# Two transformer-like layers on one core: the first modulation with its loads in another order, four column groups and products of zeros

## The chip, the cores and the metric

One Trainium2 chip, one NeuronCore of it. The metric is the device time of one execution in microseconds (us). The engines are PE (TensorE, matrix products), DVE (VectorE), ACT (ScalarE), POOL (GpSimd) and SP (SyncE, which issues all of the loads and stores here).

## The reference

A backbone of two layers over 256 context tokens and 512 latent tokens, 1024 channels each. Each layer starts with a norm whose scale and shift are computed from a conditioning vector (the modulation); four token mixers, gates, an output projection and an MLP follow. What the change touches is the first of these lines in layer 0, and the first two column blocks of the projection (the Fourier branch, fn):

```python
mod_l = (silu(c) @ ada_w[l] + ada_b[l])[:, None, :]
mod_c = (silu(c_ctx) @ ada_w[l] + ada_b[l])[None, None, :]
sh1, sc1, g1, sh2, sc2, g2 = jnp.split(mod_l, 6, axis=-1)
def rms_norm(x, w):
    return x * lax.rsqrt(jnp.mean(x * x, axis=-1, keepdims=True) + NORM_EPS) * w
def ada_rms(x, w, shift, scale):
    return rms_norm(x, w) * (1.0 + scale) + shift
hc = ada_rms(xc, norm_mix_w[l], csh1, csc1)
hl = ada_rms(xl, norm_mix_w[l], sh1, sc1)
z = h @ w_in[l]
```

## The kernel before

Activations stand transposed: eight tiles `self.x[k]` of 128 channels by 768 tokens (256 context, 512 latent). Every large product is made of three fp32r products of high and low halves, `hhi,wlo`, `hlo,whi` and `hhi,whi` (`gemm`, L311): for each of eight k it streams 256 and 512 columns. `split` (L296) makes the halves of a weight chunk, the high one on ACT and the low one on DVE. After the start the kernel is one long stream of such products on PE, through all branches of both layers; most of ada_w is not multiplied on PE but on DVE, later (`ada`, L567).

`start` (L500 to L565) is the stage in question. It computes the part of the modulation that layer 0's first norm needs, in four calls `modulation(i)` of 512 output columns each: 8 and 12 are the two halves of the scale, 0 and 4 those of the shift. A call takes eight weight tiles `adp` (128 x 512 fp32, 256 KB) from DRAM and multiplies each with two columns of `csil`, silu(c) and silu(c_ctx) of 128 channels (L514). The result, 2 x 512 in PSUM, is copied to `adt` by ACT (L516), transposed by four PE transposes (L518), and added to the bias by DVE into `mod` (L519); for the scale, `ada_fin` makes `am` of it. `mid` is a table of things to do ahead of a tile: the x tiles are loaded between the weight tiles, each followed by its square on ACT and its sum over k on POOL (`sumsq`, L597), `tables` loads constants and stores csil to DRAM as `crow` (L537, element by element), and `scalars` does the DVE work of `s5_scalars` (L1348), parameters of a later branch that are written to DRAM as `par`.

`norm_stat` (L628) sums the squares over channels by six products with a column of ones, takes a reciprocal root on DVE in eleven small steps, and spreads it over partitions by six transposes (`rs_y`). `norm_apply` (L609) then makes `hhi` (ACT) and `hlo` (DVE) per k from x, am, mod and that tile. The first two fn products (`self.head`) run on the halves k = 0 to 3 and are completed later in `fnet`, with k = 4 to 7. The first Fourier product behind them reads the constant `c_f`.

PSUM has two buffers named `b` (`pb`, L328) that the modulations and the norm share, and two named `mm`. `adp` has 16 buffers. The order of instructions on an engine is written by the framework's scheduler, starting from the order of the program; all DMAs go through SP's queue, over eight semaphores in turn, and one DMA waits for the eighth before it.

Of the kernel before, what the change touches and what calls it, by code (L numbers as in the profile page):

```python
# [10 lines left out]
F32 = mybir.dt.float32  # L11
F32R = mybir.dt.float32r
# [3 lines left out]
OP = mybir.AluOpType  # L16
# [5 lines left out]
KT = 8  # L22
# [3 lines left out]
DEPTH = 2  # L26
# [132 lines left out]
PRM_MAIN = PRM_OFF['qkk'][1]  # L159
# [56 lines left out]
class Net:  # L216
# [27 lines left out]
    def mm(self, out, a, b, start, stop):  # L244
        return self.nc.tensor.matmul(out, a, b, start=start, stop=stop)  # L245
# [59 lines left out]
    def mm3(self, out, a, b, start, stop):  # L305

        self.mm(out, a[1], b[0], start, False)
        self.mm(out, a[0], b[1], False, False)
        self.mm(out, a[0], b[0], False, stop)
# [190 lines left out]
    def start(self, sp, prm):  # L500

        nc = self.nc
        m = self.mod[0]

        def modulation(i, mid={}):

            p = self.pb()
            for k in range(KT):
                if k in mid:
                    mid[k]()  # L510
                r = sp.tile([128, 512], F32, name="adp", bufs=16)
                o, n = self.off[('adp', i, k)]
                nc.sync.dma_start(r, bass.AP(tensor=self.wst.tensor, offset=self.wst.offset + o, ap=[[n, 128], [1, n]]))
                self.mm(p[:2, :512], self.csil[:, k], r, k == 0, k == KT - 1)  # L514
            t = sp.tile([2, 512], F32, name="adt", bufs=2)
            self.act(t, p[:2, :512])  # L516
            for j in range(4):
                self.tr(p[:, 512 + 2 * j:514 + 2 * j], t[:, 128 * j:128 * j + 128], 2)  # L518
            self.tt(m[:, i:i + 4], p[:, 512:520].rearrange("p (i v) -> p i v", i=4),  # L519
                    self.main[0]['ada_b'][:, i:i + 4, None].to_broadcast([128, 4, 2]), OP.add)  # L520
            self.ada_fin(0, i, 4)

        def load():
            j = len(done)
            done.append(j)
            nc.sync.dma_start(self.x[j], self.xT[j])
            self.sumsq(sp, j, both, nc.gpsimd)

        both = [CTX, LAT]
        self.ss = {}  # L530
        done = []
        def tables():
            nc.sync.dma_start(self.ident, self.cst_ap('ident'))
            for l in range(DEPTH):
                nc.sync.dma_start(prm[l], self.prm[l][:, :PRM_MAIN])
            for v in range(2):
                nc.sync.dma_start(self.crow[v].rearrange("(k p) -> p k", p=128), self.csil[:, :, v])  # L537

        def scalars():
            for _ in range(8):  # L540
                next(later)

        later = self.s5_scalars(0, sp)
        st = []

        def stat():
            st.append(self.norm_stat(both, self.ss[0]))
            next(st[0])

        modulation(8, {2: scalars, 3: load, 5: load, 7: tables})  # L550
        modulation(0, {0: load, 2: load, 4: load, 6: load})
        self.h = self.halves()
        modulation(12, {0: load, 2: load, 6: stat})
        self.fetch(('A', 0, 'fn', 0), ('A', 0, 'fn', 1), eng=nc.vector)
        nb = next(st[0])
        modulation(4)
        self.norm_apply(0, 0, both, nb, range(4))
        self.head = []
        for j in range(2):
            self.head.append((self.pmm(), self.wk(self.chunk(('A', 0, 'fn', j)), KT)))  # L560
            self.gemm(*self.head[j], self.h, both, range(4))
        self.norm_apply(0, 0, both, self.np, range(4, 8))
        with self.tc.issue_after(self.last.ins):
            for _ in later:
                pass  # L565

# [1165 lines left out]
```

## Time and profile before

| | us |
|---|---|
| median of 3 runs | 2182.86 (2182.38 to 2184.0) |
| the profiled execution | 2183.58 |
| its span, first to last instruction | 2181.8 |
| PE busy in it | 2132.3 |
| mean granted clock of PE | 0.996 |

The span is the time from the first to the last instruction on the core; the profiled execution's time is 1.8 us longer. Busy times are sums over an engine's instructions. The clock is given as a share of PE's full 2.4 GHz; its lower level, 0.50, is 1.2 GHz.

### The profile page before, as it was taken

To read this page: it belongs to the slowest core of one execution; us is meant where nothing else is said; L and a number is where in the kernel's file an instruction comes from. 1 tells how busy PE (TensorE), PEld (TensorE's weight loads), DVE (VectorE), ACT (ScalarE), POOL (GpSimd) and SP (SyncE) were. 2 spreads that over 40 slices of the span, in tenths; PEclk is the share of its full clock that TensorE was granted. 3 is DMA by queue.
4 is the path that set the end of the run, shared out by engine and by line. 5 is a ranking of instruction groups with operands and counts; after the bars stand their busy time and mean duration, and the time that the engine had idled before them with its cause. 6 is when DMAs were issued, how large, how long until landed. Compare 5 with 4: busy or idle time off the path is not lost.

```text
span 2181.8 us, 32131 instructions
## 1 busy us (share of the span) xinstructions
PE 2132.3 (98%) x12366; PEld 1819.4 (83%) x12366; DVE 1418.9 (65%) x3303; ACT 793.7 (36%) x1346; POOL 60.9 (3%) x95
## 2 busy tenths in 40 slices
PE   6999999999999999999999999999999999999999
PEld 1888988888888888888888888997888779888887
DVE  5977789965735476667885457567646656444444
ACT  2422434564434232221222235435644544223322
POOL 2001000000000000000000001100000001000000
PEclk8999999999999999999999999999999999999999
DMA  8444233414324145445242232122144352333332
GB/s 273 148 130 131 78 103 115 144 34 130 93 73 150 36 150 159 167 134 183 100 125 82 88 118 78 40 59 80 53 123 120 112 152 60 98 96 94 96 98 94
DMA packets 117768, 239.93 MB, mean 110 GB/s; under 512 B 16208, under 2 KB 45552, under 8 KB 117616
## 3 DMA queue, kind: packets, MB, share of 16 engines
q1 hardware_dynamic: 117616, 237.89, 35.2%
q8 instruction: 97, 1.59, 0.3%
q14 instruction: 55, 0.45, 0.1%
HBM read 218.29 MB, written 19.55 MB: 109 GB/s over the span
## 4 chain that ended last, share of the span: by engine, by line
PE 79%; DVE 7%; ACT 2%; issue 2%; DMA 1%; POOL 1%; SPq 0%; POOLq 0%; ACTq 0%; DVEq 0%
PE mm L245 49%; PE b L245 27%; PE b L248 3%; DVE wlo L300 1%; DVE olo L497 1%; ACT tmp L264 1%; POOL hlo L251 0%; DVE xy L261 0%; ACT whi L299 0%; DVE ob L251 0%; DMA raws<-wst 0%; DVE gate L261 0%; DVE tmp L251 0%; DMA ohi<-crow 0%; DMA raw<-wst 0%
## 5 line engine op out<-in xcount | busy, mean ns | idle before, releaser
L245 PE MATMUL mm<-hhi,wlo 128*128 128x256 f32 (+1 forms) x1768 | 534.3, 356 | 1.1 <-DVE kr L1226 0.4
L245 PE MATMUL mm<-hlo,whi 128*128 128x256 f32 (+1 forms) x1768 | 531.5, 354 | 3.6 <-POOL hlo L251 3.5
L245 PE MATMUL mm<-hhi,whi 128*128 128x256 f32 (+1 forms) x1768 | 530.8, 354 | 0.0
L300 DVE TENSOR_TENSOR wlo<-raw,whi 128x1024 fp32r<-128x1024 f32 (+2 forms) x233 | 282.4, 1212 | 150.6 <-ACT whi L299 150.4
L245 PEld LDWEIGHTS mm<-hlo,whi 128*128 128x128 f32 x1768 | 332.2, 188 | 52.8 <-POOL hlo L251 6.5
L245 PEld LDWEIGHTS mm<-hhi,wlo 128*128 128x128 f32 x1768 | 329.8, 188 | 49.5 <-issue 1.3
L245 PEld LDWEIGHTS mm<-hhi,whi 128*128 128x128 f32 x1768 | 332.1, 188 | 46.2
L299 ACT ACTIVATE whi<-raw 128x1024 fp32r<-128x1024 f32 (+2 forms) x233 | 243.2, 1046 | 344.5 <-PE b L245 295.1
L261 DVE SCALAR_TENSOR_TENSOR xy<-b,mod,xy 128x256 f32<-128x256 f32 (+1 forms) x192 | 121.9, 659 | 147.3 <-PE b L245 147.0
L245 PE MATMUL b<-uh,wlo 128*128 128x256 f32 (+1 forms) x704 | 215.0, 359 | 2.4 <-DVE xy L261 1.3
L245 PE MATMUL b<-ul,whi 128*128 128x256 f32 (+1 forms) x704 | 214.5, 357 | 0.6 <-DVE ul L300 0.6
L245 PE MATMUL b<-uh,whi 128*128 128x256 f32 (+1 forms) x704 | 214.9, 357 | 0.0
L264 ACT ACTIVATE tmp<-mm 128x768 f32<-128x768 f32 (+3 forms) x86 | 51.5, 598 | 300.9 <-PE mm L245 281.9
L251 DVE TENSOR_TENSOR tmp<-tmp 128x768 f32<-128x768 f32 (+1 forms) x64 | 52.8, 825 | 162.0 <-ACT tmp L264 162.0
L245 PEld LDWEIGHTS b<-uh,wlo 128*128 128x128 f32 x704 | 131.2, 188 | 26.6 <-ACT uh L299 4.7
L245 PEld LDWEIGHTS b<-ul,whi 128*128 128x128 f32 x704 | 131.9, 188 | 22.3 <-DVE ul L300 1.6
L245 PEld LDWEIGHTS b<-uh,whi 128*128 128x128 f32 x704 | 132.1, 188 | 19.5
L245 PE MATMUL mm<-whi,hlo 128*128 128x256 f32 (+1 forms) x424 | 122.6, 289 | 1.1 <-DVE rpt L261 0.7
L245 PE MATMUL mm<-wlo,hhi 128*128 128x256 f32 (+1 forms) x424 | 122.1, 288 | 1.1 <-DVE wlo L300 1.1
L245 PE MATMUL mm<-whi,hhi 128*128 128x256 f32 (+1 forms) x424 | 121.9, 287 | 0.0
L264 ACT ACTIVATE gate<-mm 128x768 f32<-128x768 f32 (+1 forms) x64 | 45.0, 703 | 169.2 <-PE mm L245 168.9
L497 DVE CUSTOM_DVE_ANT_0 adu<-adr,adc 128x512 bf16<-128x512 f32 x128 | 88.2, 689 | 3.3 <-DMA adr<-wst 0.6
(454 smaller groups left out, 3183.9 us busy)
## 6 DMA issues: line engine op xcount, KB each, us to landing
raw<-wst SPq DMA_DIRECT2D x236, 512.0 KB
adr<-wst SPq DMA_DIRECT2D x96, 256.0 KB
olo<-wst SPq DMA_DIRECT2D x42, 256.0 KB
adp<-wst SPq DMA_DIRECT2D x32, 256.0 KB
raws<-wst SPq DMA_DIRECT2D x64, 128.0 KB
xy<-xT SPq DMA_DIRECT2D x16, 384.0 KB
ohi<-wst SPq DMA_DIRECT2D x22, 256.0 KB
oB<-scr SPq DMA_DIRECT2D x16, 294.0 KB
```

What stands on the lines that cost most here:

```text
L245: return self.nc.tensor.matmul(out, a, b, start=start, stop=stop)
L248: self.nc.tensor.transpose(out, a, self.ident[:n, :n])
L251: (eng or self.nc.vector).tensor_tensor(out=out, in0=a, in1=b, op=op)
L261: (eng or self.nc.vector).scalar_tensor_tensor(out, a, s, b, op0=op0, op1=op1)
L264: self.nc.scalar.activation(out, a, f, **kw)
L299: self.last_hi = self.nc.scalar.activation(hi, src, AF.Copy)
L300: return (eng or self.nc.vector).tensor_tensor(out=lo, in0=src, in1=hi.bitcast(F32), op=OP.subtract)
L497: self.nc.vector.tensor_tensor_reduce(out=junk, in0=r, in1=c[:, v], scale=1.0, scalar=0.0, op0=OP.mult, op1=OP.add, accum_out=acc[:, v:v + 1])
```

## The change

The x tiles are loaded first, then constants, the two fn weight chunks and the parameters of `s5_scalars`, then all weight tiles of the modulation. The sums of squares move from POOL to DVE. The norm's statistics are computed ahead of the modulations, in the order 8, 0, 12, 4, and between 0 and 12 `norm_apply` for k = 0 to 3 and the first half of both fn products. silu(c) is padded with zeros to 32 columns (`c32`), and tile k writes rows 32 (k mod 4) and up of PSUM; the four groups are added by a product with `sel`, four identity pieces of two columns, which also transposes. After every weight tile two fp32r products of zeros, 128 x 128 by 128 x 512, are written to an unused half of the same PSUM tile. crow is transposed on PE and stored as rows of 128 numbers, after everything else of the stage.

```diff
@@ -502,65 +502,74 @@
         nc = self.nc
         m = self.mod[0]
 
-        def modulation(i, mid={}):
+
+        c32 = sp.tile([128, KT, 32], F32, name="c32")
+        nc.gpsimd.memset(c32, 0.0)
+        self.act(c32[:, :, 0:2], self.csil)
+        sel = sp.tile([128, 2], F32, name="sel")
+        zero = sp.tile([128, 512], F32, name="zero")
+        nc.gpsimd.memset(zero, 0.0)
+        zr = sp.tile([128, 512], F32R, name="zr")
+        self.act(zr, zero)
+
+        def modulation(i):
 
             p = self.pb()
             for k in range(KT):
-                if k in mid:
-                    mid[k]()
                 r = sp.tile([128, 512], F32, name="adp", bufs=16)
                 o, n = self.off[('adp', i, k)]
-                nc.sync.dma_start(r, bass.AP(tensor=self.wst.tensor, offset=self.wst.offset + o, ap=[[n, 128], [1, n]]))
-                self.mm(p[:2, :512], self.csil[:, k], r, k == 0, k == KT - 1)
-            t = sp.tile([2, 512], F32, name="adt", bufs=2)
-            self.act(t, p[:2, :512])
+                self.last = nc.sync.dma_start(r, bass.AP(tensor=self.wst.tensor, offset=self.wst.offset + o, ap=[[n, 128], [1, n]]))
+                g = 32 * (k % 4)
+                self.mm(p[g:g + 32, :512], c32[:, k], r, k < 4, k >= 4)
+
+                for _ in range(2):
+                    self.mm(p[:, 512:], zr[:, :128], zr, True, True)
+            t = sp.tile([128, 512], F32, name="adt", bufs=2)
+            self.act(t, p[:, :512])
             for j in range(4):
-                self.tr(p[:, 512 + 2 * j:514 + 2 * j], t[:, 128 * j:128 * j + 128], 2)
+                self.mm(p[:, 512 + 2 * j:514 + 2 * j], t[:, 128 * j:128 * j + 128], sel, True, True)
             self.tt(m[:, i:i + 4], p[:, 512:520].rearrange("p (i v) -> p i v", i=4),
                     self.main[0]['ada_b'][:, i:i + 4, None].to_broadcast([128, 4, 2]), OP.add)
             self.ada_fin(0, i, 4)
 
-        def load():
-            j = len(done)
-            done.append(j)
-            nc.sync.dma_start(self.x[j], self.xT[j])
-            self.sumsq(sp, j, both, nc.gpsimd)
-
         both = [CTX, LAT]
         self.ss = {}
-        done = []
-        def tables():
-            nc.sync.dma_start(self.ident, self.cst_ap('ident'))
-            for l in range(DEPTH):
-                nc.sync.dma_start(prm[l], self.prm[l][:, :PRM_MAIN])
-            for v in range(2):
-                nc.sync.dma_start(self.crow[v].rearrange("(k p) -> p k", p=128), self.csil[:, :, v])
-
-        def scalars():
-            for _ in range(8):
-                next(later)
-
+        for k in range(KT):
+            nc.sync.dma_start(self.x[k], self.xT[k])
+            self.sumsq(sp, k, both)
+        nc.sync.dma_start(self.ident, self.cst_ap('ident'))
+        self.tt(sel, self.ident[:, 0:2], self.ident[:, 32:34], OP.add)
+        for g in (64, 96):
+            self.tt(sel, sel, self.ident[:, g:g + 2], OP.add)
+        for l in range(DEPTH):
+            nc.sync.dma_start(prm[l], self.prm[l][:, :PRM_MAIN])
+        self.fetch(('A', 0, 'fn', 0), ('A', 0, 'fn', 1))
         later = self.s5_scalars(0, sp)
-        st = []
-
-        def stat():
-            st.append(self.norm_stat(both, self.ss[0]))
-            next(st[0])
-
-        modulation(8, {2: scalars, 3: load, 5: load, 7: tables})
-        modulation(0, {0: load, 2: load, 4: load, 6: load})
+        next(later)
+        st = self.norm_stat(both, self.ss[0])
+        next(st)
+        modulation(8)
         self.h = self.halves()
-        modulation(12, {0: load, 2: load, 6: stat})
-        self.fetch(('A', 0, 'fn', 0), ('A', 0, 'fn', 1), eng=nc.vector)
-        nb = next(st[0])
-        modulation(4)
+        nb = next(st)
+        modulation(0)
         self.norm_apply(0, 0, both, nb, range(4))
         self.head = []
         for j in range(2):
             self.head.append((self.pmm(), self.wk(self.chunk(('A', 0, 'fn', j)), KT)))
             self.gemm(*self.head[j], self.h, both, range(4))
-        self.norm_apply(0, 0, both, self.np, range(4, 8))
+        modulation(12)
+        modulation(4)
+        self.norm_apply(0, 0, both, nb, range(4, 8))
+        for _ in range(7):
+            next(later)
+        p = self.pb()
+        rows = sp.tile([8, 2, 128], F32, name="crows")
+        for v in range(2):
+            self.tr(p[:8, 128 * v:128 * v + 128], self.csil[:, :, v])
+        self.act(rows, p[:8, :256])
         with self.tc.issue_after(self.last.ins):
+            for v in range(2):
+                nc.sync.dma_start(self.crow[v].rearrange("(k p) -> k p", p=128), rows[:, v])
             for _ in later:
                 pass
```

How this moves instructions shows at three places. First PE at the head of the program, before: `adp` are the weight tiles, `adt` the evicted rows, `ss` the sum of squares, `rs_y` the reciprocal root.

```order
L245 MATMUL b<-adp,csil 2x512 x8
L248 MATMUL b<-ident,adt 128x2 x4
L245 MATMUL b<-adp,csil 2x512 x8
L248 MATMUL b<-ident,adt 128x2 x4
L245 MATMUL b<-adp,csil 2x512 x6
L245 MATMUL b<-ones,ss_298 128x1 x6
L245 MATMUL b<-adp,csil 2x512 x2
L248 MATMUL b<-ident,rs_y 128x128 x4
```

And the same engine now, from its first product to the end of the first modulation (the pair of a tile and two products with `zr` stands eight times; three of them are shown, and what ends and follows them):

```order
L245 MATMUL b<-ones,ss_109 128x1 x6
L248 MATMUL b<-ident,rs_y 128x128 x6
L245 MATMUL b<-adp,c_100 32x512
L245 MATMUL b<-zr 128x512 x2
L245 MATMUL b<-adp,c_100 32x512
L245 MATMUL b<-zr 128x512 x2
...
L245 MATMUL b<-zr 128x512 x2
L245 MATMUL b<-sel,adt 128x2 x4
L245 MATMUL b<-adp,c_100 32x512
```

The norm's products now come before every modulation product, each tile is followed by two products of zeros, and four products with `sel` stand where four transposes did.

Second, PE where modulation 0 ends now, with the waits of each row (DVE_49 and Activation_49 are the counters of DVE and ACT, DMAHW those of loads):

```order
L245 MATMUL b<-sel,adt 128x2 [waits Activation_49]
L245 MATMUL b<-sel,adt 128x2 x3
L245 MATMUL b<-adp,c_100 32x512 [waits DMAHW2_49,DVE_49]
L245 MATMUL mm<-hhi_239,wlo 128x256 [waits Activation_49]
L245 MATMUL mm<-hhi_239,wlo 128x256
L245 MATMUL b<-zr 128x512
L245 MATMUL mm<-hhi_239,wlo 128x512 [waits Activation_49]
L245 MATMUL mm<-hlo_240,whi 128x256 [waits DVE_49]
```

The first tile of modulation 12 has moved ahead of the fn products and waits for DVE; the other seven stand behind the 48 fn products of k = 0 to 3. Before, all 32 tiles stood ahead of the first fn product.

Third, SP's queue: the rows around the crow stores before,

```order
L535 DMA prm_72<-prm 128x69 [waits DMAHW0_49]
L537 DMA crow<-csil 128x8x1 [waits DMAHW1_49,DVE_49]
L537 DMA crow<-csil 128x8x1 [waits DMAHW2_49]
L513 DMA adp<-wst 128x512 [waits DMAHW3_49]
L526 DMA xy_91<-xT 128x768 [waits DMAHW4_49]
L513 DMA adp<-wst 128x512 [waits DMAHW5_49]
```

and around their new place, behind all modulation tiles:

```order
L521 DMA adp<-wst 128x512 [waits DMAHW1_49,PE_49]
L270 DMA raw<-wst 128x1024 [waits DMAHW2_49,DVE_49]
L1421 DMA par_80<-par 128x1616 [waits DMAHW3_49,DVE_49]
L270 DMA raw<-wst 128x1024 [waits DMAHW4_49,Activation_49]
...
L572 DMA crow<-crows 8x128 [waits DMAHW0_49,Activation_49]
L572 DMA crow<-crows 8x128 [waits DMAHW1_49]
L465 DMA c_f_700<-cst 128x256 [waits DMAHW1_49,DMAHW0_49,DMAHW3_49,PE_49,Pool_49]
L1431 DMA par<-par_80 128x1616
```

The stores of crow have moved from between the weight tiles to just ahead of `c_f` and the load of `par`, and wait for ACT there.

## Rows read from the trace of the kernel before

**Rows 1.** The page, part 1: busy us, share of the span, instructions per engine.
```profile
PE 2132.3 (98%) x12366; PEld 1819.4 (83%) x12366; DVE 1418.9 (65%) x3303; ACT 793.7 (36%) x1346; POOL 60.9 (3%) x95
```
**Rows 2.** Windows by stage: us; PE, PEld, DVE, ACT, POOL busy; clock, DMA share, GB/s.
```profile
0.00:72.00 72.00, 54.06 (x190) 22.52 (x191) 47.83 (x211) 24.43 (x39) 13.55 (x16) 0.91 0.71 228
72.00:200.00 128.00, 123.89 (x850) 107.36 (x849) 101.83 (x311) 38.95 (x86) 3.33 (x7) 1.00 0.49 143
```
**Rows 3.** Waits of PE in 0 to 72: us in total, times, longest.
```profile
PE b L245 <- DMA adp<-wst: 15.3, 5, 8.9
```
**Rows 4.** Timeline, SP's issues and PE: start, us, engine, line, what, [idle before].
```profile
1.17 0.89 SPq L513 DMA_DIRECT2D adp<-wst  x2
...
4.23 3.57 PE L245 MATMUL b<-adp,csil 128*2 128x512 f32 x4 [4.23 <-DMA adp<-wst]
...
10.48 1.01 SPq L537 DMA_DIRECT2D crow<-csil  x2
...
16.92 5.16 SPq L513 DMA_DIRECT2D adp<-wst  x2
...
23.60 1.87 PE L245 MATMUL b<-adp,csil 128*2 128x512 f32 x2 [8.94 <-DMA adp<-wst]
```
**Rows 5.** Windows of 2 us, columns as in rows 2: clock and load rate.
```profile
24.00:26.00 2.00, 1.47 (x2) 0.00 (x0) 1.92 (x12) 0.50 (x2) 0.00 (x0) 0.50 1.00 386
...
30.00:32.00 2.00, 2.00 (x4) 0.34 (x3) 0.00 (x0) 0.49 (x2) 1.92 (x2) 0.60 1.03 390
...
36.00:38.00 2.00, 1.32 (x8) 0.49 (x7) 0.17 (x1) 1.83 (x3) 0.37 (x1) 1.00 1.05 387
```
**Rows 6.** Timeline of PE, 37 to 73.
```profile
37.14 5.31 PE L245 MATMUL b<-adp,csil 128*2 128x512 f32 x12
42.38 1.50 PE L245 MATMUL b<-ones,ss 128*128 128x1 f32 x12
43.81 1.88 PE L245 MATMUL b<-adp,csil 128*2 128x512 f32 x4
46.16 0.65 PE L248 MATMUL b<-ident,rs_y 128*128 128x128 f32 x4 [0.47 <-DVE rs_y L261]
...
47.08 0.43 PE L248 MATMUL b<-ident,rs_y 128*128 128x128 f32 x2
47.48 7.03 PE L245 MATMUL b<-adp,csil 128*2 128x512 f32 x16
54.44 0.62 PE L245 MATMUL mm<-hhi,wlo 128*128 128x256 f32 x2
54.89 0.51 PE L245 MATMUL mm<-hlo,whi 128*128 128x256 f32 x2
55.25 0.51 PE L245 MATMUL mm<-hhi,whi 128*128 128x256 f32 x2
...
72.92 1.34 PE L245 MATMUL b<-c_f,u 128*128 128x128 f32 x6
```
**Rows 7.** Timeline, the turn behind the second modulation: ACT, PE, DVE.
```profile
36.17 0.59 ACT L264 ACTIVATE adt<-b 2x512 f32<-2x512 f32 x1 [3.75 <-PE b L245]
...
36.81 0.40 PE L248 MATMUL b<-ident,adt 2*128 2x2 f32 x4 [0.68 <-ACT adt L264]
...
37.32 0.17 DVE L251 TENSOR_TENSOR mod<-b,prm 128x8 f32<-128x8 f32 x1 [8.52 <-PE b L248]
```
**Rows 8.** The page, part 6: the loads of weight tiles and their size.
```profile
adp<-wst SPq DMA_DIRECT2D x32, 256.0 KB
```
**Rows 9.** Timeline of ACT: a square, and the first eviction of hhi in both widths.
```profile
9.44 0.84 ACT L264 ACTIVATE ss<-xy 128x768 f32<-128x768 f32 x1 [6.89 <-DMA xy<-xT]
...
48.07 0.51 ACT L264 ACTIVATE hhi<-xy,mod 128x256 fp32r<-128x256 f32 x1 [0.81 <-DVE xy L261]
...
50.26 0.72 ACT L264 ACTIVATE hhi<-xy,mod 128x512 fp32r<-128x512 f32 x1 [0.73 <-DVE xy L261]
```
**Rows 10.** The page, part 5: a DVE addition over 768 columns (busy us, mean ns).
```profile
L251 DVE TENSOR_TENSOR tmp<-tmp 128x768 f32<-128x768 f32 (+1 forms) x64 | 52.8, 825 | 162.0 <-ACT tmp L264 162.0
```

## The prediction

> **What bounds the kernel now.** I read the page first: PE is busy 2132.3 us of a span of 2181.8 [rows 1], so over nearly all of the kernel the time is the length of PE's own stream of products, and any change at the start shifts the end one for one unless a later wait swallows it. The windows by stage then say where PE is not full: it is busy 54.06 of the first 72 us, but 123.89 of the next 128 [rows 2]. In the first 72 us it waits 15.3 us for modulation weights, five times [rows 3]. The timeline shows the longest: the two crow stores are issued at 10.48, two weight loads behind them stay in SP's queue for 5.16 us from 16.92, and PE takes up its products again at 23.60 after 8.94 us of idling [rows 4]. The clock windows show that idling's second price: the granted clock is 0.50 (1.2 GHz) after PE resumes, its mean in 30 to 32 is 0.60, so it rises to 1.00 (2.4 GHz) at about 31.6, and it is 1.00 later [rows 5]. From 54.44 the two fn products run, and at 72.92 the first Fourier product follows with no gap [rows 6]. That moment is my mark: all that the change does lies ahead of it, and PE's work behind it is the same in both kernels. So I work out when PE reaches it now.
>
> **The step of a modulation, part by part.** Each of the 32 weight tiles costs PE one fp32 product of 512 columns, recorded in two passes. At full clock sixteen passes take 7.03 us [rows 6]; with 0.59 as the length of a lone last pass, starts lie (7.03 - 0.59)/15 = 0.429 us apart, 0.857 us per tile. Padding silu(c) from 2 to 32 columns changes nothing in that, since the time goes with the 512 streamed columns; the weight load of 32 columns stays beside the stream.
>
> The zero products are all new. No row shows one, but the fn products are the same kind (fp32r, 128 columns of weights): a pair of 256 and 512 columns starts every 0.35 us (54.89, 55.25) [rows 6], so 512 columns take two thirds, 0.235 us. Two per tile are 0.47 us, 64 of them 15 us at full clock. They aren't hidden by a wait: a tile of 256 KB [rows 8] loads in 0.67 us at the 386 GB/s of [rows 5], and PE already needs 0.857 for it, so behind the first tiles PE is the slower side.
>
> Changing between a product that fills one strip of columns and one that fills all 128 costs too. The last pass before 42.38 starts at 37.14 + 11 x 0.429 = 41.86, so the step to the ones products is 0.52 instead of 0.43: 0.09 more. The last pass before 54.44 starts at 53.91: 0.10 more; the first pair there takes 0.45 instead of 0.35, another 0.10. Going back, the last ones product starts near 43.63 and the next pass at 43.81: 0.18 against a spacing of 0.11, 0.07 more [rows 6]. Before, a few such changes happen in all; now two per tile. A step is then 0.857 + 0.47 + 0.10 + 0.10 + 0.07 = 1.59 us. Bounds: 1.33 if the changes cost nothing (0.857 + 0.47), 1.76 if the second zero product shows its weight load too (0.10) and the way back costs twice the 0.07. I take 1.59, since its rows are products of these widths. 32 steps: 50.9 us (42.6 to 56.3), against 27.4 before.
>
> **When the steps begin.** SP now issues the eight x tiles first: 8 x 128 x 768 fp32 [rows 9] = 3.15 MB, 8.1 us at 386 GB/s. Before, the first load is issued at 1.17 and used at 4.23 [rows 4], so I let data flow from about 2.9 and the last x tile land at 11.0. Then a square of 0.84 [rows 9] and a DVE addition of 0.83 [rows 10] (it was POOL's) lead to the ones products at 12.8; from them to the transposes of the norm took 42.38 to 46.16, 3.8 us, and the six transposes 1.1 us (0.65 + 0.43) [rows 6]. PE's queue has them ahead of the first modulation step, so the steps begin at 17.7 us (16.5 to 19). By then the first five or so weight tiles have landed, and the crow stores, now rows of 128 numbers at the end of the stage, block nothing: the 8.94 us wait is gone. So is the early start at 4.23; before, a quarter of the modulation was done by 23.6.
>
> **Cold clock.** PE starts at half clock. In the trace the first four passes take 3.57 us, half speed, and the second warming goes from 23.60 to 31.6 with a turn's gap in it [rows 4, 5]: 3.6 to 8.0 us of products, of which half is lost. I take 4.6 us and so 2.3 lost (1.8 to 4.0), nearer to the first, since no gap interrupts the new stream's first eight tiles. After that I expect no loss: the clock is 1.00 around a gap of 0.68 us [rows 5, 7], and the new gaps stay below 2.
>
> **Turns between modulations.** The norm's PSUM tile now stays live from before modulation 8 to behind modulation 4, so all four share the other buffer of two: the first product of one waits for DVE's read of the last. The old chain from a modulation's end to that read: ACT from 36.17, transposes at 36.81, DVE at 37.32 for 0.17 [rows 7], 1.32 us. Four fp32 products with sel take the transposes' place, each two passes at the ones' spacing of 0.11, 0.9 us instead of 0.4. That makes 1.8 us, and the wait's start is hidden under the zeros' last 0.4 or so: about 1.6 us (1.2 to 2.0) after 8 and 12 each. After 0 and 4 the fn products also wait for hhi (0.51 us for 256 columns [rows 9]) and then for ACT, which needs 0.51 + 0.72 per k [rows 9] against PE's 3 x 0.352 = 1.06: 1.9 us after 0, where one step of 12 covers the start, 2.9 after 4, where nothing does. Sum 8.0 (6 to 10). Before, the second buffer and the steps of the next modulation covered most of it.
>
> **Work that costs nothing here.** s5_scalars' DVE work moves into the first two modulations, where DVE has nothing else but the weight splits; the crow transposes are two short products inside an ACT wait; crow, c_f and par are issued when ACT has written crows, by the sum below near 84 us, and are first needed near 95: the 128 x 1616 fp32 of par take 2.1 us at 386 GB/s. If one came late it would cost a microsecond or two, inside the range. Forty-eight pairs of fn products take 48 x 0.352 = 16.9 us as before.
>
> **Sum.** 17.7 + 2.3 + 50.9 + 16.9 + 8.0 = 95.8 us for the mark that stands at 72.92: 22.9 us later. The profiled execution took 2183.58 us, so 2206.5 by its measure; the median of the three runs is 0.7 below it: **2206 us**. A measurement tells 0.2% (4.4 us) from no change.
>
> **Rivals.**
> - *Bare steps.* The change of width is hidden by earlier weight loads and a step costs 1.33: 8.3 us less, mark at 87.5, 2198. For it: weight loads run beside products everywhere else. Against: 0.09 and 0.10 at both places [rows 6]. Chance 0.14.
> - *Column groups overlap (faster).* The four strips hold four tiles of weights at once; if a strip's 0.857 us runs beside the following products, a step falls to what the load allows, 0.67 us: 17.7 + 2.3 + 21.5 + 16.9 + 8.0 = 66.4, the mark 6.5 us earlier, 2176. It decides below (72.92 - 17.7 - 2.3 - 16.9 - 8.0)/32 = 0.875 us a step. Against it: PE's queue puts two products over all 128 columns behind every tile, and what fills every column can't run beside a strip. Nothing in the trace shows an overlap, since all tiles used one strip. Chance 0.12, of which 0.04 ends within 0.2%. The Trainium skill, TensorE: Matmul & The Clock Gate, Part 3 (Packing small matmuls), says that products in distinct column groups run at the same time (three tiles 2.38 times as fast); by that rule this rival holds. The Trainium skill, TensorEngine Tiling (Array Packing), Key Properties, says that a change of tiling mode drains TensorE; by that rule it fails here, and the 0.09 and 0.10 agree [rows 6].
> - *Longer cold.* Thin steps, or the waits at the turns, keep the clock at half for 10 us more: 5 us more, 2211. Against: passes with only 2 columns reached 1.00 at 31.6 and kept it [rows 5]. Chance 0.05.
> - *Swallowed.* DVE and the loads use the delay to run ahead and PE's 4.1 us of idling from 72 to 200 [rows 2] vanish: 2202. Chance 0.05.
>
> **Numbers.** My forecast has 0.64. The range 2194 to 2213 takes it with the bounds of its larger terms (step and turns), the bare steps, the swallowed delay and the longer cold; the faster rival's 0.12 and the far ends stay outside. Faster by over 0.2%: 0.08; within: 0.04; slower: 0.88.
>
> **What would show it.** Right: passes with zr behind each tile, a tile's start 1.5 to 1.65 us after the last at clock 1.00; no wait of 9 us for weights; first modulation product near 17.7; four turns with PE idle or on sel for over a microsecond; the first Fourier product near 96. Wrong: starts of successive tiles under 0.875 us apart, a mark near 66, or PE waiting for weights between tiles, which would hide the zeros.

## The result, and the profile after

The changed kernel takes 2219.19 us (median of four executions, 2217.33 to 2223.1) against 2183.43 us before: a ratio of 1.0166 with a 95% interval of 1.0154 to 1.0178, so 35.8 us slower. The forecast was 2206 us with a range to 2213: the direction is right, 13 us are missing.

The page's PE row says that the added time is not idling: PE is busy 34.7 us longer than in [rows 1], of a span 39.5 us longer in this execution, the slowest of the four. The two stretches of [rows 2] hold as much PE work as before, 177.9 us of 200, but at a mean clock of 0.97 behind 72 us, where it was 1.00:

```profile
PE 2167.0 (98%) x12448; PEld 1837.8 (83%) x12448; DVE 1422.7 (64%) x3313; ACT 795.1 (36%) x1349; POOL 48.8 (2%) x90
```

```profile
0.00:72.00 72.00, 52.79 (x162) 23.71 (x162) 39.44 (x181) 17.40 (x25) 0.98 (x6) 0.95 0.63 206
72.00:200.00 128.00, 125.12 (x711) 95.33 (x711) 90.94 (x264) 37.11 (x74) 0.69 (x5) 0.97 0.42 124
```

Of the waits of PE up to the mark (0 to 108 us) none is for weights any more, which held 15.3 us in [rows 3]. The two longest are these; the first, for the sum of squares, lasts from the start to 14.9 us:

```profile
PE b L245 <- DVE ss L251: 14.9, 1, 14.9
PE b L245 <- ACT adt L264: 2.6, 4, 0.7
```

PE's timeline, from the norm to the mark, answers to [rows 4, 6]:

```profile
14.92 2.72 PE L245 MATMUL b<-ones,ss 128*128 128x1 f32 x12 [14.92 <-DVE ss L251]
19.91 1.54 PE L248 MATMUL b<-ident,rs_y 128*128 128x128 f32 x6 [2.28 <-DVE rs_y L261]
21.39 1.91 PE L245 MATMUL b<-adp,c 128*32 128x512 f32 x2
...
26.82 1.04 PE L245 MATMUL b<-adp,c 128*32 128x512 f32 x2
27.80 0.73 PE L245 MATMUL b<-zr 128*128 128x512 f32 x2
28.46 1.04 PE L245 MATMUL b<-adp,c 128*32 128x512 f32 x2
...
35.01 1.05 PE L245 MATMUL b<-adp,c 128*32 128x512 f32 x2
...
37.40 1.05 PE L245 MATMUL b<-sel,adt 128*128 128x2 f32 x8 [0.69 <-ACT adt L264]
38.77 1.07 PE L245 MATMUL b<-adp,c 128*32 128x512 f32 x2 [0.31 <-DVE mod L251]
...
40.91 1.92 PE L245 MATMUL b<-adp,c 128*32 128x512 f32 x2
...
43.56 1.04 PE L245 MATMUL b<-adp,c 128*32 128x512 f32 x2
...
98.10 1.41 PE L245 MATMUL mm<-hhi,wlo 128*128 128x256 f32 x3 [0.87 <-ACT hhi L264]
...
108.01 0.38 PE L245 MATMUL b<-c_f,u 128*128 128x128 f32 x2
```

The mark stands at 108.01 in place of 72.92: 35.1 of the 39.5 us by which this execution's span is longer. The other 4.4 come behind the mark, where PE does the same work in all kernels. The profiled executions of the kernels below differ there from that of the kernel before by 2.5 us less to 4.5 us more, so 4.4 us behind the mark are not put down to the change. A tile's start follows the last by 1.64 us (26.82, 28.46): a tile 0.98, its zeros 0.66. The windows of the clock (columns as in [rows 2]) show what the forecast did not have. Behind each of the four turns it falls:

```profile
40.00:44.00 4.00, 4.00 (x7) 1.02 (x8) 4.00 (x16) 0.00 (x0) 0.00 (x0) 0.62 0.29 69
44.00:48.00 4.00, 4.00 (x11) 1.06 (x10) 0.84 (x5) 0.00 (x0) 0.00 (x0) 1.00 0.55 153
...
56.00:60.00 4.00, 4.00 (x13) 3.00 (x12) 4.00 (x10) 4.00 (x9) 0.00 (x0) 0.59 0.06 24
...
80.00:84.00 4.00, 3.67 (x10) 1.24 (x10) 3.37 (x8) 0.00 (x0) 0.00 (x0) 0.58 0.00 0
...
96.00:100.00 4.00, 2.96 (x14) 2.56 (x15) 1.96 (x5) 2.84 (x8) 0.69 (x5) 0.71 0.24 51
```

### The profile page after: what moved, and what is told of

Read it like the earlier page. It is cut to its first block, busy times and chain, and to the rows that moved or that the text cites. A ratio compares the mean times of both kernels' runs of the same rounds, so it can differ in the third digit from the quotient of the medians.

```text
span 2221.3 us, 32304 instructions
## 1 busy us (share of the span) xinstructions
PE 2167.0 (98%) x12448; PEld 1837.8 (83%) x12448; DVE 1422.7 (64%) x3313; ACT 795.1 (36%) x1349; POOL 48.8 (2%) x90
## 3 DMA queue, kind: packets, MB, share of 16 engines
q8 instruction: 98, 1.61, 0.3%
## 4 chain that ended last, share of the span: by engine, by line
PE 76%; DVE 7%; ACT 2%; issue 2%; DMA 2%; POOL 1%; SPq 0%; POOLq 0%; ACTq 0%; DVEq 0%
PE mm L245 47%; PE b L245 27%; PE b L248 3%; DVE wlo L300 1%; DVE olo L497 1%; DMA raw<-wst 1%; ACT tmp L264 1%; ACT whi L299 0%; POOL hlo L251 0%; DVE xy L261 0%; DVE ob L251 0%; DMA raws<-wst 0%; DVE gate L261 0%; DVE tmp L251 0%; POOL DT L251 0%
```

## The experiments

All kernels with their mark and their time, each against the kernel before in the same set of runs. The time is a median, the mark that of the one profiled execution. The mark moves as the time does to within 4 us, so what follows is read from the start alone, and smaller differences are read from the timeline only. (In "filled turns" the Fourier products stand in another order, and the mark cannot be compared.)

| kernel | us | to before | ratio, 95% interval | mark, us | to 72.92 |
|---|---|---|---|---|---|
| the change | 2219.19 | +35.8 | 1.0154 to 1.0178 | 108.01 | +35.1 |
| no zeros | 2179.67 | -2.5 | 0.9971 to 0.9998 | 70.72 | -2.2 |
| load order alone | 2186.49 | +4.3 | 1.0010 to 1.0029 | 76.97 | +4.1 |
| thin zeros | 2212.54 | +30.4 | 1.0128 to 1.0162 | 102.40 | +29.5 |
| filled turns | 2221.64 | +39.5 | 1.0168 to 1.0206 | - | - |
| zeros, one group | 2214.18 | +29.7 | 1.0112 to 1.0151 | 98.91 | +26.0 |
| before, crow late | 2183.11 | -1.4 | 0.9985 to 1.0007 | 73.70 | +0.8 |
| before, groups | 2192.32 | +7.8 | 1.0021 to 1.0048 | 82.81 | +9.9 |
| before, groups and crow late | 2199.14 | +14.6 | 1.0042 to 1.0084 | 85.83 | +12.9 |
| zeros by four | 2195.31 | +11.3 | 1.0039 to 1.0070 | 83.06 | +10.1 |
| turns covered | 2199.98 | +16.0 | 1.0067 to 1.0092 | 88.91 | +16.0 |
| scalars later | 2191.27 | +8.5 | 1.0027 to 1.0050 | 79.63 | +6.7 |
| groups kept whole | 2172.90 | -9.9 | 0.9948 to 0.9973 | 64.71 | -8.2 |
| fp32 zeros, other group | 2181.94 | +0.5 | 0.9989 to 1.0011 | 71.09 | -1.8 |
| fp32 zeros, first group | 2199.26 | +17.8 | 1.0057 to 1.0115 | 91.25 | +18.3 |

**No zeros.** The two products of zeros go, all else stays.

```diff
-                for _ in range(2):
-                    self.mm(p[:, 512:], zr[:, :128], zr, True, True)
```

> The change without its products of zeros; load order and four column groups stay. Theory (the products of a weight tile stand one behind another on TensorE, so the zeros are added work): a step falls from 1.64 us to the 0.86 us of one tile, the 32 steps give back 32 x 0.78 = 25 us, the first gate product moves from 108.0 to about 83 us, and the time from 2219 to about 2194 us. Rival 1 (neighbouring column groups overlap once nothing stands between them): a step takes 0.65 us or less, the first product comes at 64 to 76 us and the time is 2176 to 2187 us. Rival 2 (the zeros hold the granted clock up): more of the start runs at half the clock than the four stretches of 3.4 us of the changed kernel, and the time stays above 2202 us.

Measured: 2179.67 us, 2.5 below the kernel before, where the change is 35.8 above it. The theory (25 us back) falls, the first rival holds. PE's timeline of this run, the second and the last modulation:

```profile
30.89 3.64 PE L245 MATMUL b<-adp,c 128*32 128x512 f32 x16 [4.30 <-DVE mod L251]
...
53.65 2.49 PE L245 MATMUL b<-adp,c 128*32 128x512 f32 x16 [0.33 <-DVE mod L251]
```

Sixteen passes take 3.64 and 2.49 us, partly or wholly at the lower clock, where one group took 7.03 at the upper one [rows 6]. The four groups do run together: at full clock, four passes start within 0.02 us of one another. So the zeros cost more than their own stream: with them the overlap that the groups are there for is gone. How much of the price is their place and how much their number is read from "zeros by four" below. What the second rival names is there too, but is outweighed: up to the mark the granted clock is 0.86 on average without the zeros and 0.94 with them.

**Load order alone.** Without zeros and without groups.

```diff
-                g = 32 * (k % 4)
-                self.mm(p[g:g + 32, :512], c32[:, k], r, k < 4, k >= 4)
+                self.mm(p[:2, :512], self.csil[:, k], r, k == 0, k == KT - 1)
...
-            self.act(t, p[:, :512])
+            self.act(t, p[:2, :512])
...
-                self.mm(p[:, 512 + 2 * j:514 + 2 * j], t[:, 128 * j:128 * j + 128], sel, True, True)
+                self.tr(p[:, 512 + 2 * j:514 + 2 * j], t[:, 128 * j:128 * j + 128], 2)
```

> The new order of the loads alone: no zeros, and one group of two columns with the eviction and the transposes of the kernel before. Theory (groups bring no overlap): steps of 0.86 us as without the zeros, turns shorter by about 0.7 us each because 0.4 us of transposes stand for 1.05 us of products with sel, so 2190 to 2193 us, 1 to 4 us below the run without zeros. Rival (groups overlap): 10 us or more above the run without zeros.

Measured: 2186.49 us, 6.8 above the run without zeros; sixteen passes take 7.03 us again. Between theory and rival: the groups bring something, but not the 15 us that 32 tiles save in PE's stream, since turns are longer and the clock lower with them. The new load order by itself costs 4.3 us.

```profile
20.79 8.33 PE L245 MATMUL b<-adp,csil 128*2 128x512 f32 x16
...
31.64 7.03 PE L245 MATMUL b<-adp,csil 128*2 128x512 f32 x16 [1.44 <-DVE mod L251]
```

The first turn lasts from 29.12 to 31.64 here, 2.5 us, and the passes behind it still run at full clock.

**Thin zeros.** The same number of zeros in 32 columns, all in the first group.

```diff
-                    self.mm(p[:, 512:], zr[:, :128], zr, True, True)
+                    self.mm(p[:32, 512:], zr[:, :32], zr, True, True)
```

> The changed kernel with its zeros 32 columns wide in place of 128, so no product of the modulation changes the width. Theory (a change of width costs 0.10 us at each of the four passes' loads and is part of the 1.64 us step): a step takes 1.3 us, the first gate product comes at about 98 us, and the time is about 2209 us. Rival (the width is free and the zeros cost only their columns): a step stays at 1.64 us and the time within 2 us of 2219 us.

Measured: 2212.54 us. PE's timeline:

```profile
27.59 1.05 PE L245 MATMUL b<-adp,c 128*32 128x512 f32 x2
28.57 0.65 PE L245 MATMUL b<-zr 128*32 128x512 f32 x2
29.14 1.04 PE L245 MATMUL b<-adp,c 128*32 128x512 f32 x2
...
76.69 1.04 PE L245 MATMUL b<-adp,c 128*32 128x512 f32 x2 [0.33 <-DVE mod L251]
78.25 1.05 PE L245 MATMUL b<-adp,c 128*32 128x512 f32 x2
```

A step takes 1.55 us, 0.09 less. Neither figure held: the change of width is a small part, and a step is still a tile (0.98) and its zeros (0.58) one behind the other, though three tiles of four stand in another group than the zeros. The rest of the gain came from two half-clock stretches that did not appear in this run: behind the second and the third turn the steps are at full speed at once (76.69, 78.25), although these turns, 2.1 and 2.2 us, are as long as those of the changed kernel. Behind the first and the fourth the clock fell.

**Filled turns.** Zeros before and behind the products with sel.

```diff
             self.act(t, p[:, :512])
+            for _ in range(3):
+                self.mm(p[:, 512:], zr[:, :128], zr, True, True)
...
+            for _ in range(2):
+                self.mm(p[:, 520:], zr[:, :128], zr[:, :504], True, True)
```

> The changed kernel with five more products of zeros in each turn: three between the last tile and the products with sel, two behind these. Theory (the gap and the thin products of a turn bring the granted clock down): the four stretches of 3.4 us at half the clock, which cost about 6.5 us, do not come, the added products take 1 to 2 us of it back, and the time is 2213 to 2216 us. Rival (the clock falls for another reason, the steps themselves or the load on the chip): the stretches stay, and the time is 2219 to 2222 us.

Measured: 2221.64 us. The time looks like the rival, the trace does not. In PE's timeline behind the first turn the steps run at full speed at once:

```profile
36.94 0.96 PE L245 MATMUL b<-zr 128*128 128x512 f32 x3 [0.69 <-ACT adt L264]
37.74 0.95 PE L245 MATMUL b<-sel,adt 128*128 128x2 f32 x8
...
39.56 1.04 PE L245 MATMUL b<-adp,c 128*32 128x512 f32 x2 [0.31 <-DVE mod L251]
```

The same is true behind the third turn; behind the second and the fourth the clock fell as before (0.57 in 56 to 60 and in 100 to 104). Two stretches of some 1.5 us went, but the first three zeros began only when ACT had read the tile, so each turn grew from 2.12 to 3.38 us (36.18 to 39.56), 5 us in all. So the filled turns kept the clock up in two places of four, which leaves the cause half shown, and the price was mis-sized.

**Zeros, one group.** The zeros stay; the group of two columns, the narrow eviction and the transposes come back (the second diff above, on the changed kernel).

> The changed kernel with its zeros, but with one group of two columns, the old eviction and transposes. The runs without zeros showed four groups starting within 0.03 us of one another, and with zeros none. Theory (a product of zeros between two tiles takes the overlap away, so that the groups do nothing here): a step stays at 1.64 us, the turns fall from 2.1 to 1.5 us, fewer of the four half-clock stretches come, and the time is 2211 to 2217 us. Rival (some of the overlap survives beside the zeros): steps above 1.75 us and 2222 us or more.

Measured: 2214.18 us, the mark 9.1 us earlier than with groups. PE's timeline:

```profile
35.80 0.41 PE L248 MATMUL b<-ident,adt 2*128 2x2 f32 x4 [0.68 <-ACT adt L264]
36.52 1.02 PE L245 MATMUL b<-adp,csil 128*2 128x512 f32 x2 [0.31 <-DVE mod L251]
...
38.13 1.02 PE L245 MATMUL b<-adp,csil 128*2 128x512 f32 x2
```

A step is 1.61 us, so beside the zeros the groups win nothing and cost 0.03. The first three turns fall to 1.5 us, the last to 2.1 (2.6 us in all), and behind the first three no stretch at half clock follows. Of the 9.1 us, 0.85 is an earlier first step, 1.0 the steps, 2.6 the turns; the other 4.6 are the three stretches, 1.5 each.

**Before, crow late.** The kernel before, with the change's way to store silu(c).

```diff
-            for v in range(2):
-                nc.sync.dma_start(self.crow[v].rearrange("(k p) -> p k", p=128), self.csil[:, :, v])
...
+        with self.tc.issue_after(self.last.ins):
+            for v in range(2):
+                nc.sync.dma_start(self.crow[v].rearrange("(k p) -> k p", p=128), rows[:, v])
```

> The kernel before, with one part of the change alone: silu(c) written as rows of 128 at the end of the start, not element by element early. Theory (the 8.94 us that TensorE waited for a tile came from the two element-wise writes standing ahead of the tiles in the queues): that wait goes, the first gate product moves from 72.9 to 60 to 65 us, 2171 to 2176 us. Rival (the loads of all 32 tiles set the end of the modulations and the wait only moves): 69 to 73 us, 2179 to 2183 us.

Measured: 2183.11 us, no difference. The wait of 8.94 us for weights is gone, and another one of its size stands in its place in PE's timeline:

```profile
25.90 0.41 PE L248 MATMUL b<-ident,adt 2*128 2x2 f32 x4 [0.68 <-ACT adt L264]
35.69 7.40 PE L245 MATMUL b<-adp,csil 128*2 128x512 f32 x12 [9.38 <-DVE mod L251]
```

DVE's scalars for the scan stand ahead of `mod` in its queue and end at 35.4. The rival's end, by another wait than it named.

**Before, groups; and both parts.** The groups put into the kernel before, in the second run with crow late as well.

```diff
-                self.mm(p[:2, :512], self.csil[:, k], r, k == 0, k == KT - 1)
+                g = 32 * (k % 4)
+                self.mm(p[g:g + 32, :512], c32[:, k], r, k < 4, k >= 4)
...
```

> The kernel before with four column groups, the wide eviction and the products with sel, its load order kept, no zeros. Theory (groups run together, but the tiles' loads set the pace of the first two modulations, and only the last two, 16 tiles, shrink from 0.875 to about 0.43 us): 7 us given back, 3 us lost in four longer turns, up to 3 us at half the clock: the first gate product 2 to 6 us earlier, 2177 to 2182 us. Rival (the tiles' time on TensorE is the limit everywhere): 32 x 0.45 = 14 us less the turns, 2169 to 2173 us.

> The two parts before together: the kernel before with column groups and without zeros, and silu(c) written late as rows. Theory (without the queue's stall the tiles come at 0.65 us each from the beginning, and with groups TensorE follows them at once): the first gate product at 50 to 58 us, 2163 to 2171 us. Rival (a turn, the norm or the granted clock sets the end): no better than the better one of the two parts.

Measured: 2192.32 and 2199.14 us; both theories miss on the wrong side, and the second run is worse than either part, within what its rival says. PE then works in short pieces between tiles as they land, and the clock is at its lower level for most of 36 to 60 us. Windows of the first of the two:

```profile
36.00:42.00 6.00, 5.38 (x12) 1.19 (x8) 0.06 (x1) 0.84 (x1) 3.17 (x2) 0.59 1.04 396
42.00:48.00 6.00, 5.58 (x19) 2.74 (x18) 1.84 (x11) 0.00 (x0) 0.00 (x0) 0.50 1.06 397
...
54.00:60.00 6.00, 3.86 (x9) 1.44 (x7) 6.00 (x10) 2.56 (x5) 0.00 (x0) 0.51 0.34 102
```

In the second, PE also waits 12.6 us for `sel`, which stands behind the scalars in DVE's queue.

**Zeros by four.** The same 64 products of zeros, eight behind every fourth tile.

```diff
-                for _ in range(2):
-                    self.mm(p[:, 512:], zr[:, :128], zr, True, True)
+                if k % 4 == 3:
+                    for _ in range(8):
+                        self.mm(p[:, 512:], zr[:, :128], zr, True, True)
```

> The changed kernel with the same 64 products of zeros in another place: eight after every fourth tile in place of two after every tile. Theory (it is the place of the zeros that takes the overlap of the four groups away, their own time comes on top): four tiles take 0.9 us and eight zeros 1.8 to 2.2 us, so four tiles with their zeros 2.7 to 3.1 us in place of 6.6 us, the eight fours give back 28 to 31 us, the turns and part of the half-clock stretches stay, the first gate product at 76 to 84 us, 2188 to 2196 us. Rival (the zeros' own time is the cost wherever they stand): 6 us or more per four tiles, 2214 us or more.

Measured: 2195.31 us, 11.3 above the kernel before, the mark at 83.06. The same work in another place gives 24 us back:

```profile
25.97 1.07 PE L245 MATMUL b<-adp,c 128*32 128x512 f32 x8
26.96 2.11 PE L245 MATMUL b<-zr 128*128 128x512 f32 x8
```

Four tiles and eight zeros end 3.1 us after they begin, where the change takes 4 x 1.64 = 6.6. This settles the price: of the 38 us between the change and the run without zeros, 24 hang on the zeros' place.

**FP32 zeros, in another group and in the first.** One fp32 product of zeros per tile (two passes, as many as before), 32 columns wide; in the second run `q = 0`.

```diff
-                for _ in range(2):
-                    self.mm(p[:, 512:], zr[:, :128], zr, True, True)
+                q = (g + 64) % 128
+                self.mm(p[q:q + 32, 512:], zero[:, :32], zero, True, True)
```

> The changed kernel with one fp32 product of zeros behind each tile, 32 columns wide, in the group two further on, in place of the two fp32r products over 128 columns. Theory A (what forbids the overlap is the other number type between two tiles): all products are now fp32 in four groups, two tiles and two zeros run together, a step falls to about 0.45 us at full clock. Theory B (any product between two tiles, of whatever width, type or group, ends the overlap): tile and zeros stand one behind the other, 0.87 + 0.87 = 1.74 us a step.

> As the run with fp32 zeros in another group, but the zeros of every tile stand in the first group, where the thin fp32r zeros stood. Theory A (the number type): the first group carries ten of sixteen passes for four tiles and is the limit, about 1.07 us a step. Theory C (the thin fp32r zeros serialized only because they all stood in the first group, next to one another and before a tile): 1.5 us or more a step here, while the other run overlaps. Theory B: 1.74 us in both.

Measured: 2181.94 and 2199.26 us, steps of 0.43 and 1.07 us: as theory A has it. PE's timeline, a round of the first run and the start of the next, then the second run:

```profile
24.66 0.59 PE L245 MATMUL b<-adp,c 128*32 128x512 f32 x1
24.66 0.59 PE L245 MATMUL b<-zero 128*32 128x512 f32 x1
24.66 0.59 PE L245 MATMUL b<-adp,c 128*32 128x512 f32 x1
25.08 0.59 PE L245 MATMUL b<-zero 128*32 128x512 f32 x1
```

```profile
37.92 1.88 PE L245 MATMUL b<-zero 128*32 128x512 f32 x4
39.63 1.05 PE L245 MATMUL b<-adp,c 128*32 128x512 f32 x4
40.49 0.59 PE L245 MATMUL b<-zero 128*32 128x512 f32 x1
40.50 0.62 PE L245 MATMUL b<-adp,c 128*32 128x512 f32 x1
```

A tile and zeros start within 0.01 us of one another, also where the zeros stand in the first group, as the thin fp32r ones did. So a product between two tiles does not by itself end the overlap; the fp32r ones did, at 32 columns as at 128. The thin fp32r zeros were two products per tile and the fp32 ones a single product, with as many passes. Whether it is the mixture of the two types or fp32r alone that ends the overlap is not separated here, since no run has fp32r products in several groups; nor were fp32 zeros over all 128 columns tried, nor fp32r zeros in another group. Up to the mark the granted clock is 0.95 on average in the first of the two runs, 0.86 without zeros; the mark is 0.4 us later all the same.

**Towards a better version.** Three runs start from the one without zeros, where the first turn waited 4.30 us for DVE's scalars. The first puts the fn products and the last two modulations into each other's turns, and the scalars behind the first half of the norm:

```diff
-        modulation(12)
-        modulation(4)
...
+        modulation(12)
+        self.gemm(*self.head[0], self.h, both, range(4))
+        modulation(4)
+        self.gemm(*self.head[1], self.h, both, range(4))
...
+        with self.tc.issue_after(first.ins):
+            for _ in range(7):
+                next(later)
```

> Column groups without zeros and the changed kernel's load order, with the turns covered: the products of the third modulation stand between its tiles and those of the last, those of the second column between the last modulation and the second half of the norm, and VectorE's scalars for the scan come behind the first half of the norm. Theory (in the run without zeros 4.3 us of waiting for VectorE in the first turn, two later turns of 2.1 us and a half-clock stretch of 9 us behind them were left): the first gate product at 57 to 63 us in place of 70.7 us, 2166 to 2174 us, below both kernels. Rival (the granted clock stays at its lower level through most of the start, because the grouped modulations keep TensorE too little busy): 68 us or more, 2177 us or more.

Measured: 2199.98 us: the theory misses, and the time is the rival's for another reason. Tiles stood singly or in pairs between fp32r products, and each such piece took about 1 us (42.37, 1.04 for two passes). DVE computed the scalars until 83.2, waited for the load of `par`, and only then made `u`, for which the first Fourier product waits:

```profile
88.91 0.76 PE L245 MATMUL b<-c_f,u 128*128 128x128 f32 x2 [18.58 <-DVE u L251]
```

The second only puts the scalars behind the second modulation:

```diff
         modulation(0)
+        seen = self.seen
...
+        with self.tc.issue_after(seen.ins):
+            for _ in range(7):
+                next(later)
```

> The run without zeros (column groups, load order of the change) with one edit: VectorE's scalars for the scan come behind the second modulation's shift-and-scale values, not in the first turn. Theory (4.3 us of the first turn were TensorE waiting for VectorE, which computed these scalars): the wait falls to 0.3 us, less of the start runs at half the clock, the first gate product at 64 to 68 us in place of 70.7 us, 2173 to 2178 us. Rival (the scalars are only late somewhere else, as in the run with covered turns): 70 us or more, 2179 us or more.

Measured: 2191.27 us. The first turn's wait fell to 0.32 us, as the theory says, but PE waits 11.5 us for `u` later, which stands behind the scalars and `par` again: the rival. The third keeps each modulation's eight tiles together, computes the first scalars in the first turn and the others behind the second modulation, and gives the widest of them to GpSimd:

```diff
+        modulation(12)
+        with self.tc.issue_after(self.grp.ins):
+            self.gemm(*self.head[0], self.h, both, range(4))
+        last = self.last_mm
+        with self.tc.issue_after(last.ins):
+            modulation(4)
+        with self.tc.issue_after(self.grp.ins):
+            self.gemm(*self.head[1], self.h, both, range(4))
+        with self.tc.issue_after(seen.ins):
+            for _ in range(6):
+                next(later)
...
-        self.cmul(sp, Br, Bi, bc[:, 0], bc[:, 1], qb(qr), qb(qi), name="cb")
+        self.cmul(sp, Br, Bi, bc[:, 0], bc[:, 1], qb(qr), qb(qi), e1=e, name="cb")
```

(`grp` and `last` are PE's last tile and last fn product, `seen` is DVE's `mod` of the second modulation, and `e` is GpSimd for the first layer.)

> As the run with covered turns, but with the eight tiles of each modulation kept together on TensorE, the first scalars in the first turn, the other scalars directly behind the second modulation, and their widest products on GpSimd. Theory (tiles that stand alone between other products took 1 us each there, and the scalars behind everything else held the first gate product back by 18.6 us): the two later modulations take 2 to 3 us each in place of 20 us with their neighbours' gaps, the first gate product at 60 to 66 us, 2168 to 2177 us. Rival (VectorE, with some 35 us of norm and scalars from 20 us on, sets the end): 67 us or more, 2178 us or more.

Measured: 2172.90 us (2172.21 to 2176.05), 0.996 of the kernel before (0.9948 to 0.9973) and below both. The last modulation's sixteen passes in its timeline, and the mark:

```profile
42.95 1.93 PE L245 MATMUL b<-adp,c 128*32 128x512 f32 x16
...
64.71 0.49 PE L245 MATMUL b<-c_f,u 128*128 128x128 f32 x2 [0.31 <-DVE u L251]
```

Sixteen passes at full clock in 1.93 us, where the kernel before takes 7.03. Which of the three edits gives how much is not separated.

## Why the direction was right and the size wrong

The sum of the prediction, term by term, beside what PE's timeline shows:

| term | predicted, us | measured, us |
|---|---|---|
| first step begins | 17.7 | 21.39 |
| cold clock there | 2.3 | 2.15 |
| 32 steps | 32 x 1.59 = 50.9 | 32 x 1.64 = 52.5 |
| fn products at full clock | 16.9 | 16.9 |
| four turns | 8.0 | 2.12 + 2.14 + 2.20 + 2.73 = 9.2 |
| clock after that | 0 | the rest, 5.9 |
| mark | 95.8 | 108.0 |

- **The step** held. 1.64 us lies inside 1.33 to 1.76, and "bare steps" is out. Only the reason for one of its parts is weaker than told: with zeros of the tiles' own width the step still took 1.55, so the widths cost about 0.09 and not 0.27. The other 0.2 stays at equal width: a tile in front of fp32r zeros takes 0.98 instead of 0.86 in both runs, and the thin zeros 0.58 instead of 0.47.
- **The step that failed** is the sentence "After that I expect no loss: the clock is 1.00 around a gap of 0.68 us [rows 5, 7], and the new gaps stay below 2". The gaps did stay near 2, and yet the clock fell to half behind each of the four turns. Behind the first, two steps take 43.56 - 38.77 = 4.79 us in place of 3.28; the same loss of 1.5 us follows the second and the third, and the 24 fn pairs behind the last take 9.91 in place of 8.45. These four stretches cost the 5.9 us that the sum had at nothing. The run with one group ties them to the turns: its first three, of 1.5 us, with transposes of 0.41 in place of 1.05 us of products with sel, are followed by no such stretch, and its fourth, of 2.1 us, is. But length alone does not decide: no stretch follows two turns of 2.1 and 2.2 us with thin zeros, one of 2.5 us with the load order alone (31.64, sixteen passes in 7.03), and two of the four filled turns. What else decides is not shown. One gap of 0.68 us was no row for a gap of 2.
- **The rival "longer cold"** had this mechanism in its second half, the waits at the turns, at 5 us and with a chance of 0.05. It was priced as the only deviation; with a late start and longer turns beside it the time lay 6 us behind the range's end.
- **The start** was mis-sized by 3.7 us. The ones products begin at 14.92, not 12.8: the seven additions of squares take 0.95 to 1.04 us each on DVE, not 0.83, one behind the other, and ACT's last squares wait for them, so the chain is not the last tile's square and addition alone. From there to the first step it took 6.5 us, not 4.9, with PE's passes at half speed. ACT and DVE in their timelines:

```profile
11.63 0.85 ACT L264 ACTIVATE sq<-xy 128x768 f32<-128x768 f32 x1 [0.16 <-DVE ss L251]
```

```profile
9.58 4.15 DVE L251 TENSOR_TENSOR ss<-ss,sq 128x768 f32<-128x768 f32 x4 [1.04 <-ACT sq L264]
...
13.91 0.95 DVE L251 TENSOR_TENSOR ss<-ss,sq 128x768 f32<-128x768 f32 x1
```

- **The turns** were 1.2 us longer than the sum: the eviction also waits for the last zeros (ACT starts at 36.75, when they end), so nothing of the chain was hidden under them.
- **"Column groups overlap"** lost as forecast, but on half a reason. The Trainium skill, TensorE: Matmul & The Clock Gate, Part 3, says that products in distinct column groups run at the same time; the runs without zeros and with fp32 zeros agree (four passes start within 0.02 us, a round takes 0.43 us). The prediction held against it that a product over all columns can't run beside a strip. Thin fp32r zeros, which change no width, ended the overlap just as well, and thin fp32 ones did not. So the change's fault is not that there are zeros, but that fp32r zeros stand between the fp32 tiles.
- **Swallowed** did not come: nothing of the mark's delay of 35.1 us was gained back by the end of the profiled execution.

## What to carry to other kernels

Look at what stands between small products in distinct column groups: here eight fp32 tiles took 1.9 us together, 7.0 in one group and 13.1 with fp32r products between them, whose own part is 5.3. The filler that left the overlap whole was of the tiles' own type, 32 columns wide, and in another group than the tile ahead of it. The clock fell behind the gaps of the turns, not in the steps where the zeros stood. And when a wait goes, look for what stands next in the same queue: in "before, crow late", "turns covered" and "scalars later" it was DVE's scalars, and moving them alone only moved the wait.

## What the runs showed beyond that

- The number type of the zeros decides the overlap here: fp32 zeros of 32 columns run beside fp32 tiles (0.43 us a step), fp32r zeros of 32 columns beside none (1.55 us). Why is not shown.
- Groups alone made the kernel before slower: the clock was granted at 0.50 to 0.59 in 18 of the 24 us from 36 to 60, where the kernel before has 1.00, and the time rose by 7.8 us although tiles that stand together are cheaper. Longer turns and tiles that stand singly between fn products add to it; the parts are not separated.
- A granted clock of 1.00 in the windows does not cover the first steps: two passes take 1.91 us at 21.39, as at half clock, while the window 20 to 24 reads 1.00:

```profile
20.00:24.00 4.00, 4.00 (x10) 1.74 (x10) 3.90 (x18) 0.00 (x0) 0.00 (x0) 1.00 0.95 335
```
